# A decoder trunk on one core: the split activations xh and xl in a pool of their own at the far end of SBUF

## Chip, core and metric

The kernel runs on one core of a Trainium2 chip. A core has TensorE (PE; PEld in the profile is its weight load), VectorE (DVE), ScalarE (ACT), GpSimd (POOL) and SyncE (SP), which issues all loads here. On-chip memory (SBUF) has 128 partitions; an address in this text is a byte within each partition. PSUM holds the results of matmuls. The metric is device time in microseconds per execution; lower is better.

## What is computed

Two layers of a decoder with 256 tokens, 1024 features and float32 weights. Each layer is a macaron pair: half a SwiGLU, a token mixer, half a SwiGLU. The mixer of the first layer is attention over dilated windows, that of the second latent attention.

```python
def swiglu(x, w_in, w_out):
    gate, up = jnp.split(x @ w_in, 2, axis=-1)
    return (jax.nn.silu(gate) * up) @ w_out

# each layer
x += 1/2 SwiGLU1(rms(x)); x += mixer(rms(x)); x += 1/2 SwiGLU2(rms(x))
```

`w_in` is 1024 x 5632, `w_out` 2816 x 1024, four of each. The weights are read once; the profile counts 194.14 MB read from HBM.

## The kernel before

Activations stay in SBUF, features on partitions: `xT[p, kt, token]` holds feature kt*128 + p, with KT = 8 chunks of 256 tokens. A product with weights runs as three passes in float32r, since weights and activations are each split into a high and a low part: weights into hi and lo (`piece`, lines 71 to 89: SP loads 1 MB into one of four raw buffers, ACT writes hi, DVE writes lo = raw - hi; three hi and three lo buffers of 8 KB per partition take turns), the activations into xh and xl (`split_x`, lines 100 to 115: ACT writes xh, line 115 on DVE writes xl). xh and xl are two tiles of 8 KB per partition that live through the whole kernel; every layer writes them anew.

Lines 95 to 97 are the three passes: hi with xh, hi with xl, lo with xh. Each matmul has a stationary operand of 128 x 128 (loaded by LDWEIGHTS) and a moving one of 128 x 256.

```python
 64 self.xg = self.xp.tile([P, GCOLS + KT * S], F32, name="xg")
 67 self.xh = self.xp.tile([P, KT, S], F32R, name="xh")
 68 self.xl = self.xp.tile([P, KT, S], F32R, name="xl")
...
 94 for i, (wh, wl, xh, xl) in enumerate(terms):
 95     self.nc.tensor.matmul(out, wh, xh, start=start and i == 0, stop=False, **kw)
 96     self.nc.tensor.matmul(out, wh, xl, start=False, stop=False, **kw)
 97     self.nc.tensor.matmul(out, wl, xh, start=False, stop=stop and i == n - 1, **kw)
...
180 for k in range(KT):
181     for u in range(2):
182         self.mm3(
183             ps[:, u * S : (u + 1) * S],
184             [(hv[:, k, u, :], lv[:, k, u, :], self.xh[:, k, :], self.xl[:, k, :])],
...
432 nc.tensor.matmul(o, self.xh[:, k, ts], hi[:, k, :], start=k == 0, stop=False)
```

- **FFN** (`ffn`, lines 170 to 245). `up(c)` for 22 chunks: 48 matmuls with the weights stationary and xh, xl moving, into a PSUM tile of pool wk (lines 180 to 184). `gate(c)` makes the hidden part h and splits it into hh and hl (pool hh, six buffers each of 1 KB). `down(c)`: 24 matmuls with hh, hl moving, into the PSUM pool acc; two of them follow every second up. `closing` (line 247) ends the down product bank by bank, each followed by the residual and the next split of x.
- **Dilated layer** (`dilated`, line 391): q and k products (lines 418 to 420) with xh, xl stationary and 512 columns of weights moving; v products (lines 432 to 434) with xh, xl stationary and 256 columns moving, into acc; attention; and an output product through lines 95 to 97 with oth, otl moving (`out_product`, line 367), into acc.
- **Latent layer** (`latent`, line 586): an input product through lines 95 to 97 with xh, xl moving, then products from the tiles ch and cl, attention, and an output product with its own oth, otl.

Pools take SBUF in the order in which they are opened, from the low end: const, xp (with xg, xh, xl), raw, hi, lo, st, and behind them the pools of the layer that runs. The Tile framework records the instructions, orders them on each engine and sets the semaphores.

Of the kernel before, what the change touches and what calls it, by code (L numbers as in the profile page):

```python
"""Two-layer hybrid decoder trunk (dilated-window attention, latent attention) on one core.

Activations stay on chip, feature-major: xT[p, kt, token] holds feature kt*128+p.  Products of
float32 operands against the weights run as three float32r passes over an exact split
w = hi + lo (12 significant bits each): hi*xh + hi*xl + lo*xh.  RMS-norm scales are applied
after the products (per token), so a product never waits for a norm's statistics.

The tokens stand even ones first, then odd ones: a dilation of 4 or 16 never joins the two
halves, so those groups' scores are two diagonal blocks.  Only inside the latent layer are they
in their own order, which its input's split and its output's residual turn to and from.  # L10
"""
# [11 lines left out]
F32R = mybir.dt.float32r  # L23
# [6 lines left out]
P = 128  # L30
S = 256
D = 1024
KT = D // P
# [17 lines left out]
class Trunk:  # L51
    def __init__(self, ctx, tc):
        self.tc, self.nc = tc, tc.nc
        e = ctx.enter_context
        self.const = e(tc.tile_pool(name="const", bufs=1))
        self.xp = e(tc.tile_pool(name="xp", bufs=1))
        self.rawp = e(tc.tile_pool(name="rawp", bufs=4))
        self.hip = e(tc.tile_pool(name="hip", bufs=3))
        self.lop = e(tc.tile_pool(name="lop", bufs=3))
        self.st = e(tc.tile_pool(name="st", bufs=2))  # L60
        self.acc = e(tc.tile_pool(name="acc", bufs=4, space=PSUM))
        self.wk = e(tc.tile_pool(name="wk", bufs=3, space=PSUM))
        self.ob = e(tc.tile_pool(name="ob", bufs=1, space=PSUM))
        self.xg = self.xp.tile([P, GCOLS + KT * S], F32, name="xg")
        self.gains = self.xg[:, :GCOLS]
        self.xT = self.xg[:, GCOLS:].rearrange("p (k s) -> p k s", k=KT)
        self.xh = self.xp.tile([P, KT, S], F32R, name="xh")
        self.xl = self.xp.tile([P, KT, S], F32R, name="xl")

    # ---- weights: load a piece, split it exactly into two float32r parts  # L70
    def piece(self, src, cuts=1, before=None):
        """cuts: parts the split is made in; before: called ahead of each part's load, else it's one load."""
        nc = self.nc
# [17 lines left out]
    def mm3(self, out, terms, start, stop, **kw):  # L91
        """out += sum over (wh, wl, xh, xl) of w x; the weight is stationary."""
        n = len(terms)
        for i, (wh, wl, xh, xl) in enumerate(terms):
            self.nc.tensor.matmul(out, wh, xh, start=start and i == 0, stop=False, **kw)  # L95
            self.nc.tensor.matmul(out, wh, xl, start=False, stop=False, **kw)  # L96
            self.nc.tensor.matmul(out, wl, xh, start=False, stop=stop and i == n - 1, **kw)  # L97

    # ---- residual stream
    def split_x(self, d0, xs, in_order=False, shared=False):  # L100
        """Gained x (chunks from d0) as float32r pairs, with the tokens even|odd or in their own order;
        shared: ScalarE and VectorE take turns at the high parts."""
        nc = self.nc
# [13 lines left out]
    def squares(self, d0, xs, in_order=False):  # L117
        """The sum of squares over the chunks."""
        nc = self.nc
# [15 lines left out]
    def residual(self, d0, n, acc, scale, in_order=False):  # L135
        """x += scale * acc for n chunks from d0; acc is their part of a bank, its tokens maybe in order."""
        xs = self.xT[:, d0 : d0 + n, :]
# [9 lines left out]
    def stats(self):  # L147
        """Per-token mean square + eps and its inverse root."""
        nc = self.nc
# [8 lines left out]
    def spread_rstd(self):  # L158
        """The inverse root along the free axis, on every partition."""
        nc = self.nc  # L160
# [7 lines left out]

    # ---- SwiGLU
    def ffn(self, up_w, out_w, finish, start=None, started=None, hook=None):  # L170
# [76 lines left out]
    def closing(self, parts, down, accs, finish, scale):  # L247
        """The last terms of a product bank by bank, each followed by its chunks' residual and split."""
        for d0, cs in parts:
            for c in cs:  # L250
                down(c, (d0, d0 + 1))
            if d0 < KT - 2:
                finish(d0, 2, accs[d0 // 2], scale)
            else:
                for i in range(2):
                    finish(d0 + i, 1, accs[d0 // 2][:, i * S : (i + 1) * S], scale)

    # ---- tables
    def setup_first(self):
# [6 lines left out]
        nc.gpsimd.memset(self.mhalf, -0.5)  # L266
        # the activation table and the PE's clock warm up while the first loads run
        nc.scalar.activation(self.st.tile([P, 2], F32, name="warm"), self.mhalf[:, :2], AF.Silu)
# [4 lines left out]
    def setup(self, cst, pos, gtab):  # L273
        """Masks, and rotary tables with the gains: two token tiles even|odd, two in their own order."""
        nc = self.nc
# [27 lines left out]
        nc.scalar.activation(cos, n, AF.Sin)  # L303
        # A: q gain 0:64, k gain 64:128; B: q gain 128:224, k gain 224:320
        self.tA = k.tile([P, NTT, 2, DA], F32, name="tA")
        self.tB = k.tile([P, NTT, 2, 2, 32], F32, name="tB")
        for tt in range(NTT):
            for qk, sc in ((0, DA**-0.5), (1, 1.0)):
                for hf in range(2):
# [7 lines left out]
                    )  # L317
        # latent attention: q over 96 features, and k's rotary part over 32
        self.tAq = k.tile([P, NTT, QKB], F32, name="tAq")
# [3 lines left out]
        for tt in range(NTT):  # L323
            sc = QKB**-0.5
            # k's gain over the features that aren't rotated goes to q's side of the scores
            nc.vector.scalar_tensor_tensor(
# [12 lines left out]

    # ---- softmax of one score block: probabilities, divided by their sum  # L340
    def softmax(self, p, s, mask):
# [11 lines left out]
    def transposed(self, pool, p, n, name):  # L353
        """n 128-blocks of p, each transposed, in SBUF."""
        nc = self.nc
# [11 lines left out]
    def out_product(self, w_out, oth, otl):  # L367
        """Steps of the output product: part(k, banks)."""
        ws = {}
# [19 lines left out]

    # ---- dilated windows  # L390
    def dilated(self, qk_w, v_w, w_out, finish):
        nc, tc = self.nc, self.tc
        with (
# [63 lines left out]
            def attention(hq, qt, kt, v):  # L457
                """Pipelined steps over (pair of heads, token tile): scores, turned probabilities, outputs."""
                ps, pts, obs = {}, {}, {}
# [54 lines left out]
            for hq in range(4):  # L514
                # group 0's scores are 256 wide: float32r pairs
                qt, kt = (
# [36 lines left out]
    def norm_rope_a(self, at, ps, tt, ee):  # L553
        """Heads of q and k (4 + 4, 64 wide): RMS norm with gains, then rotary embedding."""
        nc = self.nc
# [28 lines left out]

    # ---- latent attention
    def latent(self, in_w, kv_w, q_w, w_out, finish):
        nc, tc = self.nc, self.tc
        with (
# [10 lines left out]
            def in_product(pc):  # L599
# [12 lines left out]
                for i in range(2):  # L612
                    # chunks 0,1: kv rank; 2,3,4: q rank; the rotary key (32 features) comes third
                    c = (0, 1, None, 2, 3, 4)[pc * 2 + i]
# [32 lines left out]
            def mean_square(cs, name):  # L647
                """Per token: mean square of a rank's features + eps, in units of the unscaled ones."""
                ps = self.ob.tile([P, 512], F32, name="ob")
# [16 lines left out]
            def rotary_key():  # L666
                """Token-major: r_x kr', gained and rotated; its square sum."""
                ps = self.ob.tile([P, 512], F32, name="ob")
# [126 lines left out]
    def tok_product(self, out, xh, xl, chunks, tt, wp, cols):  # L795
        """Token-major product: the activations' chunk is stationary."""
        nc = self.nc
# [94 lines left out]

# ---- host: layouts of the inputs, and constants of the shapes
def _layout(i):
# [11 lines left out]
    a["gtab"] = c(np.broadcast_to(gt, (P, gt.size)))  # L906
    # [4, ff chunk, p, (kt, gate|up, 128)]
    w = i["ffn_w_in"].reshape(4, KT, P, 2, NC_FF, P)
    a["up"] = c(w.transpose(0, 4, 2, 1, 3, 5).reshape(4, NC_FF, P, PIECE))
    w = i["ffn_w_out"].reshape(4, NC_FF // 2, 2, P, D)  # L910
    a["down"] = c(w.transpose(0, 1, 3, 2, 4).reshape(4, NC_FF // 2, P, PIECE))
    # [q|k|v][group][quarter][256]
    w = i["a_w_in"][0].reshape(KT, P, 3, GA, 4, S)
# [9 lines left out]
    a["b_out"] = c(i["b_w_out"][0].reshape(4, 2, P, D).transpose(0, 2, 1, 3).reshape(4, P, PIECE))  # L923
    # constants
    ms = []
# [38 lines left out]
```

## Time and profile before

| what | value |
|---|---|
| runs | median 1181.53 us of 3 (1181.19, 1181.53, 1183.71) |
| profiled execution | span 1178.2 us (no other time of it is listed) |
| PE, PEld | busy 1159.9 us (98%), 1106.9 us (94%), 9142 each |
| DVE, ACT, POOL | busy 792.3, 593.1, 102.6 us |
| loads | 196.59 MB, mean 167 GB/s |
| granted TensorE clock | mean 0.998 |

The span runs from the first instruction to the last. Matmuls overlap in the profile: a row of some 280 ns starts some 120 ns behind the one before it, so busy time and mean durations of PE don't say how often one starts. The timeline does, which lists instructions by their start.

### The profile page before, as it was taken

The page shows a single profiled execution, that of the slowest core. Times are in us where ns is not written, and L with a number is a line of the kernel's source. Part 1 is how long each engine was busy: PE and PEld are TensorE (multiplying, and loading weights), DVE is VectorE, ACT ScalarE, POOL GpSimd, SP SyncE. Part 2 cuts the span into 40 slices and gives each one's busy share as a digit, 9 for nine tenths or more (in the row PEclk, how much of TensorE's full clock was granted, in tenths as well). Part 3 has the DMA queues.
Part 4 walks back from the last instruction along what each step waited for, and adds up shares of the span by engine and source line. Part 5 has one row for each costly group of instructions (what it writes and reads, how often), then busy time and mean ns, then how long its engine had stood idle before and what let it go on. Part 6 is the DMA issues. An engine that isn't in the chain of part 4 may idle for free.

```text
span 1178.2 us, 21736 instructions
## 1 busy us (share of the span) xinstructions
PE 1159.9 (98%) x9142; PEld 1106.9 (94%) x9142; DVE 792.3 (67%) x1384; ACT 593.1 (50%) x980; POOL 102.6 (9%) x98
## 2 busy tenths in 40 slices
PE   7999999999999999999999999999999899999998
PEld 7999999888888888999999999999998789999998
DVE  6855557979777776675555676555576897655554
ACT  6444445556555555654444454444466875444441
POOL 2000001212111111200000020000013212000000
PEclk9999999999999999999999999999999999999999
DMA  8655554554444344155555545555533235455540
GB/s 319 216 182 191 191 186 144 214 179 144 141 146 144 112 158 142 56 215 179 184 184 189 192 182 179 179 179 183 184 129 122 108 110 184 175 183 191 192 149 37
DMA packets 29042, 196.59 MB, mean 167 GB/s; under 512 B 3344, under 2 KB 3856, under 8 KB 5904
## 3 DMA queue, kind: packets, MB, share of 16 engines
q1 hardware_dynamic: 28944, 195.21, 47.4%
q8 instruction: 71, 1.16, 0.4%
q14 instruction: 27, 0.22, 0.1%
HBM read 194.14 MB, written 1.05 MB: 166 GB/s over the span
## 4 chain that ended last, share of the span: by engine, by line
PE 90%; DVE 6%; ACT 2%; issue 1%; POOL 1%; DMA 1%; SPq 0%; DVEq 0%; POOLq 0%
PE wk L96 14%; PE wk L97 14%; PE wk L95 14%; PE acc L95 9%; PE acc L97 9%; PE acc L96 9%; PE acc L418 3%; PE acc L420 3%; PE acc L419 3%; PE wk L358 1%; PE acc L432 1%; PE acc L434 1%; DVE lo L88 1%; PE acc L433 1%; PE ob L491 1%; PE wk L446 1%
## 5 line engine op out<-in xcount | busy, mean ns | idle before, releaser
L88 DVE TENSOR_TENSOR lo<-raw,hi 128x512 fp32r<-128x512 f32 (+2 forms) x408 | 447.0, 1119 | 213.2 <-ACT hi L87 211.6
L87 ACT CAST hi<-raw 128x512 fp32r<-128x512 f32 (+2 forms) x408 | 375.2, 963 | 277.2 <-PE wk L96 172.9
L95 PE MATMUL wk<-xh,hi 128*128 128x256 f32 x1408 | 399.8, 284 | 1.6 <-ACT hi L87 1.6
L97 PE MATMUL wk<-xh,lo 128*128 128x256 f32 x1408 | 399.0, 283 | 1.8 <-DVE lo L88 1.8
L96 PE MATMUL wk<-xl,hi 128*128 128x256 f32 x1408 | 398.8, 283 | 0.1
L97 PEld LDWEIGHTS wk<-xh,lo 128*128 128x128 f32 x1408 | 269.9, 192 | 2.6 <-DVE lo L88 2.6
L95 PEld LDWEIGHTS wk<-xh,hi 128*128 128x128 f32 x1408 | 270.1, 192 | 2.2 <-ACT hi L87 2.1
L96 PEld LDWEIGHTS wk<-xl,hi 128*128 128x128 f32 x1408 | 270.0, 192 | 0.8 <-DVE xl L115 0.5
L95 PE MATMUL acc<-hh,hi 128*128 128x256 f32 x704 | 197.2, 280 | 0.0
L97 PE MATMUL acc<-hh,lo 128*128 128x256 f32 x704 | 196.4, 279 | 0.0
L96 PE MATMUL acc<-hl,hi 128*128 128x256 f32 x704 | 196.4, 279 | 0.0
L95 PEld LDWEIGHTS acc<-hh,hi 128*128 128x128 f32 x704 | 132.3, 188 | 0.0
L97 PEld LDWEIGHTS acc<-hh,lo 128*128 128x128 f32 x704 | 132.3, 188 | 0.0
L96 PEld LDWEIGHTS acc<-hl,hi 128*128 128x128 f32 x704 | 131.9, 187 | 0.0
L204 ACT CAST hh<-h 128x256 fp32r<-128x256 f32 x88 | 35.4, 406 | 168.2 <-DVE h L201 168.0
L195 DVE TENSOR_TENSOR gu<-wk,bc 128x512 f32<-128x512 f32 x88 | 60.5, 691 | 76.5 <-PE wk L97 76.2
L418 PE MATMUL acc<-hi,xh 128*128 128x512 f32 x192 | 76.6, 399 | 0.0
L419 PE MATMUL acc<-lo,xh 128*128 128x512 f32 x192 | 75.2, 392 | 0.0
L420 PE MATMUL acc<-hi,xl 128*128 128x512 f32 x192 | 74.9, 390 | 0.0
L205 DVE TENSOR_TENSOR hl<-h,hh 128x256 fp32r<-128x256 f32 x88 | 37.1, 424 | 33.2 <-ACT hh L204 33.1
L562 POOL TENSOR_TENSOR rr<-r,mhalf 128x8 f32<-128x8 f32 x24 | 39.2, 1636 | 205.2 <-DVE r L560 205.2
L130 POOL TENSOR_TENSOR ssq<-sq 128x256 f32<-128x256 f32 x6 | 4.8, 796 | 596.3 <-ACT sq L127 422.0
(183 smaller groups left out, 1521.3 us busy)
## 6 DMA issues: line engine op xcount, KB each, us to landing
raw<-in_up SPq DMA_DIRECT2D x87, 1024.0 KB, 4.8
raw<-in_down SPq DMA_DIRECT2D x44, 1024.0 KB, 4.8
raw<-in_a_qk SPq DMA_DIRECT2D x24, 1024.0 KB, 4.8
raw<-in_a_v SPq DMA_DIRECT2D x12, 1024.0 KB, 4.8
raw<-in_a_out SPq DMA_DIRECT2D x4, 1024.0 KB, 5.4
raw<-in_b_out SPq DMA_DIRECT2D x4, 1024.0 KB, 4.9
raw<-in_b_in SPq DMA_DIRECT2D x3, 1024.0 KB, 4.9
raw<-in_b_q SPq DMA_DIRECT2D x4, 576.0 KB, 3.6
```

The source lines that it names most:

```text
L87: nc.scalar.copy(hi[:, c], raw[:, c])
L88: nc.vector.tensor_tensor(lo[:, c], raw[:, c], hi.bitcast(F32)[:, c], op=ALU.subtract)
L95: self.nc.tensor.matmul(out, wh, xh, start=start and i == 0, stop=False, **kw)
L96: self.nc.tensor.matmul(out, wh, xl, start=False, stop=False, **kw)
L97: self.nc.tensor.matmul(out, wl, xh, start=False, stop=stop and i == n - 1, **kw)
L195: nc.vector.tensor_tensor(gu, ps.rearrange("p (u s) -> p u s", u=2), self.bc.unsqueeze(1).broadcast_to([P, 2, S]), op=ALU.mult)
L204: nc.scalar.copy(hh, h)
L205: nc.vector.tensor_tensor(hl, h, hh.bitcast(F32), op=ALU.subtract)
L418: nc.tensor.matmul(pss[tt], xh, hi[:, k, :], start=kk == 0, stop=False)
L419: nc.tensor.matmul(pss[tt], xh, lo[:, k, :], start=False, stop=False)
L420: nc.tensor.matmul(pss[tt], xl, hi[:, k, :], start=False, stop=kk == KT - 1)
L562: nc.gpsimd.tensor_tensor(rr, r8, self.mhalf[:, :8], op=ALU.pow)
```

## The change

xh and xl move from the pool xp, where they stood behind xg, to a new pool `far` with one buffer, which takes its memory from the far end of the partition (`side="right"`). Comments and docstrings are blanked too, which does nothing; lines behind 67 have their numbers raised by two.

```diff
         self.xT = self.xg[:, GCOLS:].rearrange("p (k s) -> p k s", k=KT)
-        self.xh = self.xp.tile([P, KT, S], F32R, name="xh")
-        self.xl = self.xp.tile([P, KT, S], F32R, name="xl")
+
+        self.far = e(tc.tile_pool(name="far", bufs=1, side="right"))
+        self.xh = self.far.tile([P, KT, S], F32R, name="xh")
+        self.xl = self.far.tile([P, KT, S], F32R, name="xl")
```

Each engine has the same instructions in the same order, with the same waits, before and after. The two built programs differ in addresses (first byte of each buffer within a partition):

| tile | before | after |
|---|---|---|
| const pool, xg | 16512 to 36351 | the same |
| xh | 36352 | 212960 |
| xl | 44544 | 221152 |
| raw (4) | 52736, 60928, 69120, 77312 | 36352, 44544, 52736, 60928 |
| hi (3) | 85504, 93696, 101888 | 69120, 77312, 85504 |
| lo (3) | 110080, 118272, 126464 | 93696, 101888, 110080 |
| hh (6) | 152384 to 158527 | 136000 to 142143 |
| hl (6) | 158528 to 164671 | 142144 to 148287 |
| oth, otl of the dilated layer | 211776, 219968 | 195392, 203584 |
| oth, otl of the latent layer | 188224, 196416 | 171840, 180032 |

[...] PSUM places don't change.

## Rows read from the trace of the kernel before

**Rows 1.** The page's first line, and PE in its part 1 (busy us, share, instructions).
```profile
span 1178.2 us, 21736 instructions
PE 1159.9 (98%) x9142; PEld 1106.9 (94%) x9142; DVE 792.3 (67%) x1384; ACT 593.1 (50%) x980; POOL 102.6 (9%) x98
```

**Rows 2.** The page's part 4: the chain that ended last, by engine and line.
```profile
PE 90%; DVE 6%; ACT 2%; issue 1%; POOL 1%; DMA 1%; SPq 0%; DVEq 0%; POOLq 0%
PE wk L96 14%; PE wk L97 14%; PE wk L95 14%; PE acc L95 9%; PE acc L97 9%; PE acc L96 9%; PE acc L418 3%; PE acc L420 3%; PE acc L419 3%; PE wk L358 1%; PE acc L432 1%; PE acc L434 1%; DVE lo L88 1%; PE acc L433 1%; PE ob L491 1%; PE wk L446 1%
```

**Rows 3.** Waits, ACT's longest: total us, times, longest.
```profile
ACT hi L87 <- PE wk L96: 172.9, 75, 4.3
```

**Rows 4.** Windows: stretch, us, then busy us by engine, clock, DMA share, GB/s.
```profile
core 0: us, PE busy (x) PEld busy (x) DVE busy (x) ACT busy (x) POOL busy (x), PEclk, DMA share, GB/s
0.00:20.00 20.00, 13.88 (x83) 12.51 (x83) 11.03 (x22) 12.34 (x22) 7.03 (x14) 1.00 0.87 317
20.00:190.00 170.00, 170.00 (x1427) 170.00 (x1426) 108.13 (x156) 73.71 (x83) 0.00 (x0) 1.00 0.57 198
```

**Rows 5.** Groups by form: xcount | busy us, mean ns | idle before.
```profile
L95 PE MATMUL wk<-xh,hi 128*128 128x256 f32 x1408 | 399.8, 284 | 1.6 <-ACT hi L87 1.6
...
L95 PEld LDWEIGHTS wk<-xh,hi 128*128 128x128 f32 x1408 | 270.1, 192 | 2.2 <-ACT hi L87 2.1
...
L95 PE MATMUL acc<-hh,hi 128*128 128x256 f32 x704 | 197.2, 280 | 0.0
...
L95 PEld LDWEIGHTS acc<-hh,hi 128*128 128x128 f32 x704 | 132.3, 188 | 0.0
...
L418 PE MATMUL acc<-hi,xh 128*128 128x512 f32 x192 | 76.6, 399 | 0.0
...
L432 PE MATMUL acc<-hi,xh 128*128 128x256 f32 x192 | 55.3, 288 | 0.0
...
L95 PE MATMUL acc<-oth,hi 128*128 128x256 f32 x128 | 37.4, 296 | 0.7 <-DVE kn L818 0.7
...
L95 PE MATMUL acc<-xh,hi 128*128 128x256 f32 x48 | 13.8, 288 | 0.0
```

**Rows 6.** Timeline of PE, a down and two up products: start us, us, instruction.
```profile
122.58 0.28 PE L95 MATMUL acc<-hh,hi 128*128 128x256 f32 x1
...
127.88 0.29 PE L95 MATMUL wk<-xh,hi 128*128 128x256 f32 x1
...
128.60 0.28 PE L95 MATMUL wk<-xh,hi 128*128 128x256 f32 x1
...
139.16 0.28 PE L96 MATMUL wk<-xl,hi 128*128 128x256 f32 x1
```

**Rows 7.** Windows in the up product of rows 6, columns as in rows 4.
```profile
128.60:130.20 1.60, 1.60 (x16) 1.60 (x15) 0.30 (x1) 1.26 (x1) 0.00 (x0) 1.00 1.01 425
130.20:131.80 1.60, 1.60 (x16) 1.60 (x15) 1.60 (x1) 0.00 (x0) 0.00 (x0) 1.00 0.28 118
```

**Rows 8.** Timeline of PE in a v product.
```profile
216.00 0.28 PE L434 MATMUL acc<-hi,xl 128*128 128x256 f32 x1
...
219.24 0.28 PE L434 MATMUL acc<-hi,xl 128*128 128x256 f32 x1
```

**Rows 9.** Timeline of PE in the dilated layer's output product.
```profile
478.44 0.28 PE L95 MATMUL acc<-oth,hi 128*128 128x256 f32 x1
...
480.56 0.28 PE L95 MATMUL acc<-oth,hi 128*128 128x256 f32 x1
```

**Rows 10.** Timeline of PE, a later chunk of the same output product.
```profile
484.89 0.28 PE L97 MATMUL acc<-oth,lo 128*128 128x256 f32 x1
...
485.91 0.28 PE L97 MATMUL acc<-oth,lo 128*128 128x256 f32 x1
```

**Rows 11.** Timeline of PE in a q and k product.
```profile
220.75 0.39 PE L418 MATMUL acc<-hi,xh 128*128 128x512 f32 x1
...
224.15 0.39 PE L418 MATMUL acc<-hi,xh 128*128 128x512 f32 x1
```

**Rows 12.** Groups by form: the instructions that write xl.
```profile
L115 DVE SCALAR_TENSOR_TENSOR xl<-xg,xh 128x256 fp32r<-128x256 f32 x48 | 28.8, 635 | 3.9 <-ACT xh L114 3.9
```

## The prediction

> **What bounds the kernel now.** I read the page from the top. The span is 1178.2 us and TensorE (PE) is busy for 1159.9 us of it [rows 1]. That alone doesn't make PE the bound, so I went to the chain that ended last: 90% of it is PE, and its three longest pieces are lines 95, 96 and 97, the three passes of a product [rows 2]. Then the waits: what ScalarE (ACT) waits for most before it splits a weight piece is PE, to give a `hi` buffer back (172.9 us), so the split stands behind PE and not ahead of it [rows 3]. [...] The time of this kernel is therefore the number of matmuls times the distance from one start to the next, and that distance is what is to be read.
>
> The groups by form give the counts; each form stands there once for its three passes. With 256 moving columns and xh or xl as an operand there are 3 x 1408 in the FFN up products, 3 x 192 in the v products (there xh is the stationary operand) and 3 x 48 in the latent input product, **4944** in all. With hh or hl there are 3 x 704 = 2112, with oth or otl 3 x 128 = 384. With 512 moving columns and xh stationary there are 3 x 192 = 576 [rows 5]. The durations of the matmuls in these rows (280 to 399 ns) overlap and can't be added; only starts tell.
>
> In a down product the starts run from 122.58 to 127.88 us in 45 steps: 5.30/45 = 117.8 ns. In the up products behind it they run from 128.60 to 139.16 us in 88 steps: 10.56/88 = 120.0 ns [rows 6]. The v products, with xh stationary, start 120 ns apart as well: 216.00 to 219.24 us in 27 steps [rows 8]. The output product of the dilated layer, with oth moving, is of the quicker kind: 478.44 to 480.56 us in 18 steps, 117.8 ns [rows 9]. Both kinds take turns through the same three hi and three lo buffers, and read 128 weights and 256 columns on 128 partitions at the same clock. The up product writes another PSUM pool than the down product, but the v product writes the same one and still takes 120. Other engines don't explain it either: in two neighbouring windows of the up stretch DVE goes from 0.30 to 1.60 of 1.60 us and the DMA engines from their full share to 28%, and the 120 ns go on through both [rows 6, 7]. What the slow ones share is xh and xl. Even a weight load is longer beside xh: 192 against 188 ns, from the same hi buffers [rows 5]. One chunk of the output product goes faster still, 484.89 to 485.91 us in 9 steps, 113.3 ns [rows 10]. So three paces are on record, and the middle one belongs to operands that lie elsewhere in memory.
>
> **The change part by part.** By the built programs no instruction is added, removed or moved on any of the five queues (SP's and POOL's among them), and every wait is on the same semaphore with the same value. Only addresses differ. xh goes from byte 36352 to 212960 of each partition, xl from 44544 to 221152; const and xg stay; everything behind them moves down by 16384 bytes, so raw, hi, lo, hh and oth keep their places relative to each other. Before, xh and hi started at the same place modulo 512 bytes, while hh and oth stood 320 bytes off; after, xh stands 480 off, and at 32 modulo 64, where every operand of PE stood at 0 modulo 64 until now. Before, xh and xl were also the only operands of any product with weights below byte 85504. So the change takes away both things that set the slow kind apart, the place and the common offset.
>
> - *The 4944 matmuls with xh or xl.* No row shows xh at its new place. The nearest rows are those of hh and oth, which have the same shape, weights and roles [rows 6, 9]; the oth of rows 9 lies from byte 211776 on, right where xh will be. I take their pace: 120.0 - 117.8 = 2.2 ns less, x 4944 = **10.9 us**. The bounds are 113.3 ns [rows 10], 6.7 ns less, 33.1 us, and on the other side one such step more, 126.7 ns, 33.1 us lost.
> - *The 576 with 512 columns.* They start 226.7 ns apart (220.75 to 224.15 us in 15 steps) [rows 11], 13.3 over the 213.3 ns of their columns. No row shows this form at another pace; between nothing and 576 x 2.2 = 1.3 us, taken as 0.
> - *The 2112 + 384 with hh and oth.* They move down together with hi and lo: 0, as nothing between the operands changes. Bound: back to 120, 2496 x 2.2 = 5.5 us lost.
> - *Writing xh and xl.* The same instructions at other addresses; line 115 has 48 of 635 ns [rows 12]: 0. A tenth more on each would be 3.0 us, most of it beside PE's work.
> - *What could be late next.* An up chunk of 48 steps shrinks from 5.76 to 5.65 us. By rows 4 DVE has 36% of the stretch to spare, ACT 57% and the DMA engines 43%, so no wait takes the gain. In the first 20 us, where PE waits for loads (83 matmuls), 0.2 us of it is lost.
>
> Sum: 10.9 us off. It is made on the profiled execution, whose span is 1178.2 us; that is 3.3 below the median of the runs, 1181.53, and I leave this difference as it is: 1181.5 - 10.9 = **1170.6 us**.
>
> **The rivals.**
>
> *No change (1181.5).* The 120 belongs to something else in these products, or xh falls into it wherever it lies. For it: 120 is 13.3 ns over the 106.7 ns of 256 columns, and the 512-column form is the same 13.3 over its own [rows 11], so 13.3 may be the common toll and 117.8 the exception. Against it: the same hi buffers are read at two paces, and xh and xl alone tell them apart. [...] Chance 0.27.
>
> *Slower, by the new offset (1214.6).* xh and xl will be the only operands that start in the middle of a 64-byte block. [...] If PE is fed by such blocks, 256 columns now touch 17 of them: 4944 x 6.7 = 33.1 us more. It decides as soon as one extra block isn't hidden in the 13.3 ns that a step has beyond its columns. [...] Against it: those 13.3 ns. [...] Chance 0.13.
>
> *Slower, by place (1187.0).* The low addresses are slow for whoever lies there. The hi buffers now begin at 69120 instead of 85504, nearer to where xh was. If the border lies between, x stays at 120 because of its weights, and hh and oth fall to 120 too: 5.5 us more. Chance 0.09.
>
> *Much faster (1148.4).* xh falls into the 113.3 pace: 33.1 us off. For it: rows 10; against it: oth holds that pace in this short stretch only. Chance 0.09.
>
> **How the numbers follow.** A measurement of this kernel can tell some 0.2% (2.4 us) from no change. The forecast has 0.42 and is the likeliest. Faster: 0.42 + 0.09 = 0.51; same: 0.27; slower: 0.13 + 0.09 = 0.22. The range takes in the forecast (its own range is 1168 to 1173: the wide form's 1.3 us below, a fifth of the gain lost above), no change and the smaller slowdown, 0.78 together. Downwards it reaches to 1159, half way to the 113.3 pace, for mixtures of the two. Left out are 126.7 throughout and 113.3 throughout.
>
> **What would show it.** In the profile after, starts in an up product 117.8 ns apart and the weight load beside xh at 188 ns, with down products unchanged: right, and the span about 11 us shorter with the same counts. At 120 and 192: no change. At 127: the offset. Down products at 120: the place. The forecast is wrong as well if the up products quicken and the span doesn't, through idle time of PE in front of lines 95 and 97.

## The result and the profile after

The changed kernel takes **1174.83 us** (median of 4 runs, 1173.87 to 1175.84) against 1181.36 us for the kernel before in the same series: a ratio of 0.9944, 95% interval 0.9927 to 0.9960. That is 6.5 us faster. The forecast was 1170.6 us, with a range from 1159 to past the smaller slowdown of 1187.0: the sign and the place of the gain were right, its size was too large (10.9 us).

The page of the profiled execution (its time 1175.65 us), the first line and PE in part 1. Line numbers are two higher than before.

```profile
span 1173.9 us, 21736 instructions
PE 1154.4 (98%) x9142; PEld 1097.8 (94%) x9142; DVE 793.6 (68%) x1384; ACT 593.0 (51%) x980; POOL 102.9 (9%) x98
```

The counts are those of [rows 1]. DVE and ACT have the same busy time to within 1.3 us; only PE and its weight load lost some. So what changed is how often a matmul starts. The groups by form (xcount | busy us, mean ns | idle before):

```profile
L97 PEld LDWEIGHTS wk<-xh,hi 128*128 128x128 f32 x1408 | 266.5, 189 | 1.8 <-ACT hi L89 1.7
L97 PEld LDWEIGHTS acc<-hh,hi 128*128 128x128 f32 x704 | 132.3, 188 | 0.0
L420 PE MATMUL acc<-hi,xh 128*128 128x512 f32 x192 | 77.6, 404 | 0.0
```

Against [rows 5] the weight load beside xh fell from 192 to 189 ns, beside hh it stayed at 188. The 512-column matmul of the q and k products grew from 399 to 404 ns. The timeline of PE (start us, us, instruction) gives the distances: first and last row of a stretch of down products, of the up products behind it, of a q and k product and of the v product behind that.

```profile
122.65 0.28 PE L97 MATMUL acc<-hh,hi 128*128 128x256 f32 x1
...
128.19 0.28 PE L99 MATMUL acc<-hh,lo 128*128 128x256 f32 x1
128.30 0.28 PE L97 MATMUL wk<-xh,hi 128*128 128x256 f32 x1
...
139.54 0.28 PE L99 MATMUL wk<-xh,lo 128*128 128x256 f32 x1
...
206.17 0.40 PE L420 MATMUL acc<-hi,xh 128*128 128x512 f32 x1
...
212.94 0.40 PE L422 MATMUL acc<-hi,xl 128*128 128x512 f32 x1
...
213.75 0.29 PE L435 MATMUL acc<-lo,xh 128*128 128x256 f32 x1
...
219.12 0.28 PE L436 MATMUL acc<-hi,xl 128*128 128x256 f32 x1
```

- Up: 11.24 us in 95 steps, **118.3 ns** where [rows 6] had 120.0.
- Down: 5.54 us in 47 steps, 117.9 ns, as in [rows 6].
- v: 5.37 us in 46 steps, 116.7 ns where [rows 8] had 120.
- q and k: 6.77 us in 29 steps, **233.4 ns** where [rows 11] had 226.7.

Over the whole trace, pauses left out, the means went from 119.99 to 118.28 ns (up), from 119.81 to 116.96 (v), from 119.8 to 118.3 (latent input), from 227.9 to 233.3 (q and k) and from 117.86 to 117.73 (down). Times the numbers of matmuls: 4224 x 1.71 = 7.2, 576 x 2.85 = 1.6, 144 x 1.5 = 0.2 and 2112 x 0.13 = 0.3 us gained, 576 x 5.4 = 3.1 us lost. The sum is 6.2 us of the measured 6.5.

### The profile page after: what moved, and what is told of

It reads as the page before. It is cut to its first block, busy times and chain, and to the rows that moved or that the text cites. A ratio compares the mean times of both kernels' runs of the same rounds, so it can differ in the third digit from the quotient of the medians.

```text
span 1173.9 us, 21736 instructions
## 1 busy us (share of the span) xinstructions
PE 1154.4 (98%) x9142; PEld 1097.8 (94%) x9142; DVE 793.6 (68%) x1384; ACT 593.0 (51%) x980; POOL 102.9 (9%) x98
## 4 chain that ended last, share of the span: by engine, by line
PE 89%; DVE 7%; ACT 2%; POOL 1%; issue 1%; DMA 1%; SPq 0%; DVEq 0%; POOLq 0%; ACTq 0%
PE wk L98 14%; PE wk L99 14%; PE wk L97 14%; PE acc L97 9%; PE acc L99 9%; PE acc L98 9%; PE acc L420 3%; PE acc L422 3%; PE acc L421 3%; DVE lo L90 2%; PE acc L434 1%; PE wk L360 1%; PE acc L436 1%; PE acc L435 1%; PE ob L493 1%; ACT hi L89 1%
## 5 line engine op out<-in xcount | busy, mean ns | idle before, releaser
L99 PEld LDWEIGHTS wk<-xh,lo 128*128 128x128 f32 x1408 | 266.5, 189 | 3.3 <-DVE lo L90 3.3
L97 PEld LDWEIGHTS wk<-xh,hi 128*128 128x128 f32 x1408 | 266.5, 189 | 1.8 <-ACT hi L89 1.7
L98 PEld LDWEIGHTS wk<-xl,hi 128*128 128x128 f32 x1408 | 266.3, 189 | 0.9 <-DVE xl L117 0.6
```

## The experiments

**Place or offset.** The change moves xh to another place and, with it, to another offset from hi: xh stood 0 bytes behind hi modulo 512 and stands 480 behind it now. Three kernels and a scan take the two apart.

*far_0*: the changed kernel with padding in its pool, so that the place stays and the offset goes back to 0.

```diff
         self.far = e(tc.tile_pool(name="far", bufs=1, side="right"))
         self.xh = self.far.tile([P, KT, S], F32R, name="xh")
         self.xl = self.far.tile([P, KT, S], F32R, name="xl")
+        self.pad = self.far.tile([P, 120], F32, name="pad")
```

> xh and xl stay at the far end, but start 480 bytes lower (212480), so that they begin at the same place modulo 512 as hi and lo, as they did before the change. Place theory (the low end of SBUF was slow): up products keep the quicker pace of about 118.3 ns, time as after the change, about 1174.8 us. Offset theory (equal starts modulo 512 lock the step at 120 ns): up products back at 120.0 ns and 192 ns per weight load, time back at about 1181.4 us.

Measured: 1181.34 us, ratio 1.0000 (0.9991 to 1.0009). Timeline of PE, up products of far_0:

```profile
130.79 0.29 PE L98 MATMUL wk<-xh,hi 128*128 128x256 f32 x1
...
142.19 0.28 PE L100 MATMUL wk<-xh,lo 128*128 128x256 f32 x1
```

11.40 us in 95 steps are 120.0 ns again. At the new place and the old offset nothing is gained, so the place is worth nothing.

*near_480* and *near_320*: the kernel before with xh and xl where they were, moved by padding of 480 or 320 bytes, and the rest of 512 behind them. Their diff, for 480 (80 and 48 for near_320):

```diff
+        self.pad = self.xp.tile([P, 120], F32, name="pad")
         self.xh = self.xp.tile([P, KT, S], F32R, name="xh")
         self.xl = self.xp.tile([P, KT, S], F32R, name="xl")
+        self.pad2 = self.xp.tile([P, 8], F32, name="pad2")
```

> xh and xl stay in their old pool at the low end, with 480 bytes of padding ahead and 32 behind, so that they stand 480 bytes off hi and lo modulo 512, as after the change. Place theory: up products stay at 120.0 ns, about 1181.4 us. Offset theory: up products at about 118.3 ns, v products at about 117, q and k products slowed to some 231 ns, time about 1174.8 us.

> xh and xl at the low end, 320 bytes off hi and lo modulo 512, which is where hh and oth stand and where they took 117.8 ns before. Place theory: 120.0 ns, 1181.4 us. Offset theory: up products at 117.8 ns, 0.5 ns less than after the change, which over 4224 matmuls is 2 us: about 1173 us, if the q and k products don't slow further.

Measured: near_480 1175.33 us, ratio 0.9954 (0.9941 to 0.9966); near_320 1172.48 us, ratio 0.9929 (0.9916 to 0.9941). Timelines of PE, up products, first of near_480, then of near_320:

```profile
128.03 0.28 PE L97 MATMUL wk<-xh,hi 128*128 128x256 f32 x1
...
139.26 0.28 PE L99 MATMUL wk<-xh,lo 128*128 128x256 f32 x1
```

```profile
127.68 0.28 PE L97 MATMUL wk<-xh,hi 128*128 128x256 f32 x1
...
138.87 0.28 PE L99 MATMUL wk<-xh,lo 128*128 128x256 f32 x1
```

95 steps take 11.23 us (118.2 ns) and 11.19 us (117.8 ns). Without the new pool, 480 bytes give the changed kernel's paces, and 320, the offset that hh and oth had all along, gives their 117.8 ns. The offset is the cause. (hi starts at 0 modulo 512 bytes in all these kernels, so that the offset is also xh's own address modulo 512; *mixed_offsets* below takes these two apart in part.)

*offset_scan*: streams of 96 matmuls in the forms of the kernel, each behind a short pause, at 19 offsets and, for the up form, at ten places of its moving operand.

> A kernel of matmul streams alone, none of the model's work: the forms of the up, v and q/k products, each with 96 (48 for 512 columns) matmuls from idle, for 19 offsets of xh and xl against hi and lo (0 to 480 in steps of 32, and 8, 16, 48), then the up form at 10 places across SBUF with offsets 0 and 480. Offset theory: 120.0 ns at offset 0 at every place, other values at other offsets, the same at every place; at 480 about 118.3 (up), 117 (v), 231 (q/k, against 226.7 at 0). Place theory: the pace depends on the place, and not on the offset. If only starts off a 64-byte multiple matter, 32, 96, 160 and so on differ from 64, 128, 192.

In its timeline each stream is one row (start us, length us, form, count, pause ahead). First the up form at 96, 192, 256 and 320, then the q and k form with its stationary operand at 0, 32, 64 and 192, then the up form at offsets 0 and 480 at the lowest and at the highest of the ten places:

```profile
53.47 11.79 PE L43 MATMUL ps<-z 128*128 128x256 f32 x96 [0.73 <-ACT res L40]
...
90.76 11.16 PE L43 MATMUL ps<-z 128*128 128x256 f32 x96 [0.73 <-ACT res L40]
...
115.01 11.78 PE L43 MATMUL ps<-z 128*128 128x256 f32 x96 [0.73 <-ACT res L40]
...
139.71 11.15 PE L43 MATMUL ps<-z 128*128 128x256 f32 x96 [0.73 <-ACT res L40]
...
481.55 11.20 PE L43 MATMUL ps<-z 128*128 128x512 f32 x48 [0.52 <-ACT res L40]
493.48 11.47 PE L43 MATMUL ps<-z 128*128 128x512 f32 x48 [0.73 <-ACT res L40]
505.68 11.47 PE L43 MATMUL ps<-z 128*128 128x512 f32 x48 [0.73 <-ACT res L40]
...
554.47 11.26 PE L43 MATMUL ps<-z 128*128 128x512 f32 x48 [0.73 <-ACT res L40]
...
712.19 11.78 PE L43 MATMUL ps<-z 128*128 128x256 f32 x96 [0.73 <-ACT res L40]
724.70 11.62 PE L43 MATMUL ps<-z 128*128 128x256 f32 x96 [0.73 <-ACT res L40]
...
935.87 11.78 PE L43 MATMUL ps<-z 128*128 128x256 f32 x96 [0.73 <-ACT res L40]
948.38 11.62 PE L43 MATMUL ps<-z 128*128 128x256 f32 x96 [0.73 <-ACT res L40]
```

The place does nothing: 11.78 and 11.62 us at both ends. The offset does, and 256 is as slow as 0. Over the second half of each stream the up form takes 120.0 ns at 0 and 256, but 119.9 to 120.1 at 96, 352 and 8 too, so a common offset isn't the only slow one. It takes 113.3 at 192 and 320, 118.4 at 224 and 480, and between 116.6 and 118.7 at all others. The v form takes 120.0 at 0 and 256, at 160 and 416 too, and 115.6 (at 8) to 118.6 elsewhere. The q and k form is best at 0 and 256, where the others are among their worst: 226.7 ns there, 228.7 at 192 and 448, 230.6 to 234.1 elsewhere. VectorE does nothing from the second stream on, and ScalarE only copies out between streams: in 9.6 us within the streams at 192 and 256 (from 92.0 and from 116.0 us) PE runs 87 and 82 matmuls, VectorE, ScalarE and GpSimd are busy for 0.00 us, and the DMA share is 0.01. The effect needs no other engine: it lies in the places of PE's own two operands.

**Which offset is worth having.** *near_192* and *near_256* are near_320 with other padding (48 and 80 float32, 64 and 64).

> xh and xl stay at the near end, 192 bytes behind hi modulo 512 (48 float32 of padding ahead of xh, 80 behind xl; nothing else moves by other than 512 bytes). Theory of the offset, by the scan of matmuls alone: up products at 117.8 ns or, if they hold the quicker of two paces, 113.3; v products 117.8; q and k products 228.8 instead of 226.7. Sum from 1181.4: 4224 x 2.2 + 576 x 2.2 - 576 x 2.1 = 9.3 us less, 1172 us; with the up products at 113.3 it would be 1153. If only the far offsets 320 and 480 help and 192 does not, the up products stay at 120 and the time at 1181 or, with the slower q and k products, 1182.5.

> As near_192, with xh and xl 256 bytes behind hi modulo 512 (64 float32 of padding on either side). If what counts is the offset modulo 256, this is a common offset again: up and v products 120.0, q and k products 226.7, the time of the kernel before, 1181.4 within 2. If any offset other than 0 modulo 512 helps, up products at 118 to 119 and the time 1174 to 1178.

Measured: near_192 **1155.22 us**, ratio 0.9784 (0.9769 to 0.9800); near_256 1181.15 us, ratio 0.9995 (0.9985 to 1.0005). The windows show two stretches of 120 us, in the first and in the third FFN; what counts is PE's (x...), the matmuls that run in it, those begun just before it among them. Columns are as in [rows 4]. The kernel before and near_256, each in the first FFN, then near_192 in both:

```profile
60.00:180.00 120.00, 120.00 (x1008) 120.00 (x1007) 68.46 (x63) 49.91 (x50) 0.00 (x0) 1.00 0.53 184
```

```profile
60.00:180.00 120.00, 120.00 (x1008) 120.00 (x1007) 68.44 (x63) 49.98 (x49) 0.00 (x0) 1.00 0.54 185
```

```profile
60.00:180.00 120.00, 120.00 (x1021) 120.00 (x1021) 68.61 (x64) 51.20 (x50) 0.00 (x0) 1.00 0.55 187
720.00:840.00 120.00, 120.00 (x1046) 120.00 (x1045) 71.54 (x66) 51.49 (x52) 0.00 (x0) 1.00 0.56 191
```

An offset of 256 gains nothing: 1008 matmuls, as before. At 192 the first FFN does 1021, with its up products at 117.7 ns, and the third does 1046, with its up products at 113.4, at the same clock of 1.00 and with the same addresses. So the offset alone doesn't fix the pace; at 192 two are possible, and something else chooses. (This trace is of the slowest of near_192's four executions, 1158.92 us. The other three took 1154.88 to 1155.54; no row shows their first FFN, which may have run at the other pace.)

*pace_memory* asks what.

> Leaves the whole network out: only streams of matmuls, its output is not the reference's. Streams of 96 up-like matmuls (256 columns, offsets between moving and stationary operand of 0, 64, 192, 320, 448, 480 bytes modulo 512) follow one another without idle time, in pairs; at 192 and 320 also from idle, with down-like streams, and after single matmuls of other widths. If the pace belongs to the offset alone, every stream at 192 and 320 runs at 113.3 ns, as from idle in the offset scan, whatever ran before it. If the pace is a state that is carried over, streams at 192 and 320 run at 113.3 after some predecessors and at 117.8 after others, and a single matmul of another width between two streams may change it.

Windows of pace_memory (columns as above): a stream at 192 behind one at 0, one at 192 behind one at 64, and one at 192 behind one at 320.

```profile
49.00:58.60 9.60, 9.60 (x87) 9.60 (x86) 0.00 (x0) 0.00 (x0) 0.00 (x0) 1.00 0.01 2
...
139.00:148.60 9.60, 9.60 (x84) 9.60 (x83) 0.00 (x0) 0.00 (x0) 0.00 (x0) 1.00 0.01 2
...
240.00:249.60 9.60, 9.60 (x87) 9.60 (x87) 0.00 (x0) 0.33 (x1) 0.00 (x0) 1.00 0.01 2
```

By their starts, 87 in a window are a pace of 113.3 ns and 84 one of 117.8. Every stream at 192 right behind one at 0 ran at 113.3, the one behind 64 at 117.8 to its end. The one stream at 320 in the scan, behind a pause, ran at 113.3; here, without such pauses, streams at 320 ran at 117.8 in all but one case. So the pace is a mode: past its first few matmuls each stream kept its own, 113.3 or 117.8 ns, to its end. What a single matmul of another width between two streams does to the mode is not shown.

*all_192* is near_192 with a third padding, a pool of 96 float32 behind `st`, by which hh, hl, oth and otl also stand at 192. *all_192_reset* adds 16 matmuls at offset 0 in the first FFN:

```diff
                     wo(c // 2)
+                    if c == 5 and start:
+                        for _ in range(16):
+                            nc.tensor.matmul(accs[3][:, :S], wos[0][0][:, 0, S : S + P], wos[0][0][:, 0, :S], start=True, stop=True, skip_group_check=True)
                     if c < NC_FF - 1:
                         down(c - 3)
```

> near_192 with a further 96 float32 (384 bytes) of padding behind the pool st, so that hh, hl, oth and otl too stand 192 bytes behind hi and lo modulo 512 instead of 320. Theory (offset sets which paces are possible, and which of the two holds is carried on from one matmul to the next): down products at 113.4 ns in the FFNs whose up products have that pace, 4.4 ns x 528 less in each, three of four in near_192: 7 us less than near_192's 1155.2, 1148; 1142 if the first FFN falls into 113.3 as well, 1164 and more if a second one stays at 117.8 throughout. Rival (the pace belongs to the role of hh, or each stretch chooses afresh): down products stay at 117.8 and the time at 1155.

> all_192 with 16 more matmuls in the first FFN, ahead of its first down product, whose two operands both come from one hi buffer, 0 bytes apart modulo 512; their result is overwritten. 16 x 120 ns = 1.9 us more work. If the pace is carried on and a stretch at offset 0 throws it back, as every stream at 192 behind one at 0 ran at 113.3 in the run of streams, the first FFN goes on at 113.4 instead of 117.8 behind them: some 864 up and 528 down matmuls x 4.4 = 6.1 us less, 4 us net below all_192 if that one's first FFN stays at 117.8, and 2 us above it if it doesn't. If the pace is chosen afresh at each stretch, 2 us above all_192 in any case.

Measured: all_192 1164.64 us, ratio 0.9855 (0.9840 to 0.9870); all_192_reset 1169.51 us, ratio 0.9898 (0.9881 to 0.9914). (The 16 matmuls of all_192_reset change what one accumulator holds; the number and form of all others are those of all_192.) Windows of all_192 (early in the first FFN, then the two stretches), of all_192_reset (the first two of these), and timeline of its 16 matmuls:

```profile
24.00:47.00 23.00, 23.00 (x205) 23.00 (x204) 20.84 (x71) 12.83 (x23) 0.00 (x0) 1.00 0.77 286
60.00:180.00 120.00, 120.00 (x1062) 120.00 (x1061) 71.30 (x65) 52.47 (x51) 0.00 (x0) 1.00 0.56 194
720.00:840.00 120.00, 120.00 (x1021) 120.00 (x1021) 69.80 (x64) 50.23 (x49) 0.00 (x0) 1.00 0.54 185
```

```profile
24.00:47.00 23.00, 23.00 (x198) 23.00 (x197) 20.04 (x70) 9.68 (x18) 0.00 (x0) 1.00 0.76 279
60.00:180.00 120.00, 119.94 (x1018) 119.74 (x1017) 70.09 (x65) 50.43 (x50) 0.00 (x0) 1.00 0.56 193
```

```profile
47.18 0.87 PE L243 MATMUL acc<-hi 128*128 128x256 f32 x6
...
48.33 0.76 PE L243 MATMUL acc<-hi 128*128 128x256 f32 x5
...
54.35 0.77 PE L243 MATMUL acc<-hi 128*128 128x256 f32 x5
```

My forecast of 1148 us for all_192 fell by sign: it is 9 us slower than near_192. But it shows the mode plainly. Now all products of an FFN have one offset, and from its first down product on a whole FFN runs in one mode: the first at 113.3, up and down alike, the other three at 117.8. In near_192 the down products, at 320 and 117.8 ns, had stood between the up products without spoiling them in three FFNs of four.

The reset tested less than it was meant to. Its 16 matmuls did not run as one stretch, but as groups of 6, 5 and 5 with up products between them, behind the first down products and not ahead of them; the mode stayed at 117.8. But another thing came out. Ahead of the first group PE has the same 314 matmuls in the same order in both kernels, from the same addresses, and yet from 24 us on all_192 ran them at 113.3 ns and all_192_reset at 117.8. So the matmuls and their addresses together don't fix the mode either.

**A combination without the slow mode.** *mixed_offsets* gives the three passes offsets of their own.

> Leaves the whole network out: only streams of up-like matmuls, its output is not the reference's. The three passes get offsets of their own (hi with xh, hi with xl, lo with xh): 20 combinations, each as a stream of 96 behind 48 at offset 64 (which left 192 at 117.8 ns in the run before) and again behind 48 at offset 0 (which left it at 113.3). Then 48 at 64, 48 at 192, n at 0 for n from 1 to 96, and 96 at 192. If the pace is a mode that is carried on, 192 throughout runs at 117.8 behind 64 and at 113.3 behind 0, and some length of n is needed to change it: 16 did not do it in all_192_reset, so more than 16 here. If a mixed combination breaks the mode, it runs at one pace behind both: at 113.3 it would be worth having in the kernel, at 117.8 or above not.

Windows of mixed_offsets: first 192 for both passes with hi and 64 for the pass with lo, behind a stream at 64 and behind one at 0; then 128 for the pass with lo, behind 64; then 192 throughout, behind 2 and behind 16 matmuls at 0.

```profile
53.00:62.60 9.60, 9.60 (x87) 9.60 (x86) 0.00 (x0) 0.02 (x1) 0.00 (x0) 1.00 0.00 0
69.50:79.10 9.60, 9.60 (x87) 9.60 (x87) 0.00 (x0) 0.19 (x1) 0.00 (x0) 1.00 0.00 0
86.00:95.60 9.60, 9.60 (x84) 9.60 (x83) 0.00 (x0) 0.26 (x1) 0.00 (x0) 1.00 0.00 0
...
727.50:737.10 9.60, 9.60 (x84) 9.60 (x84) 0.00 (x0) 0.00 (x0) 0.00 (x0) 1.00 0.01 2
...
797.40:807.00 9.60, 9.60 (x87) 9.60 (x86) 0.00 (x0) 0.27 (x1) 0.00 (x0) 1.00 0.01 2
```

Of 20 combinations only (192, 192, 64) and its like (192, 192, 320), besides 192 throughout, ran at 113.3 behind both predecessors. 192 throughout behind 64 ran at 113.3 eight times and at 117.8 twice, so its choice isn't made by the predecessor's offset alone. Behind 8 or more matmuls at 0 it ran at 113.3 in all six cases, behind 1, 2 or 4 at 117.8. My expectation of more than 16 took the 16 of all_192_reset for one stretch; its groups of 5 and 6 lie between the 4 and the 8 of this run and don't contradict it. What chooses the mode stays open.

The combinations also show that the weights' address counts, and not that of xh alone: with xh and xl in place and only lo moved, (192, 192, 64) ran at 113.3 ns and (192, 192, 128) at 118.0 to 118.5. That only the difference of the two addresses counts, and not each one's own place modulo 512, is not shown: hi keeps one place modulo 512 in all runs. Nor do good offsets add up: (192, 320, 320) took 120 to 122 ns.

*lo_shift* puts (192, 192, 64) into the kernel: all_192 with lo moved by 128 bytes.

```diff
+        self.lgap = e(tc.tile_pool(name="lgap", bufs=1))
         self.lop = e(tc.tile_pool(name="lop", bufs=3))
...
-        self.pad3 = self.gap.tile([P, 96], F32, name="pad3")
+        self.pad3 = self.gap.tile([P, 64], F32, name="pad3")
+        self.pad4 = self.lgap.tile([P, 32], F32, name="pad4")
```

> all_192 with lo alone moved by 128 bytes (32 float32 of padding ahead of it, 32 fewer behind st): hi with xh and hi with xl stay 192 bytes apart modulo 512, lo with xh becomes 64, and the same for hh and oth. In the run of mixed offsets this combination ran at 113.3 ns behind both predecessors, 64 and 0, with the same steps each time. If it breaks the mode that holds 117.8, the up and down products of all four FFNs run at 113.3: 4752 matmuls of the later three FFNs x 4.45 = 21 us less than all_192, 1143 to 1144; the v, q and k products, whose moving operand changes its offset with lo, can move this by 3 either way. If the streams alone mislead (the other engines or the pauses of the kernel matter), one or more FFNs stay at 117.8: 7 us more for each, 1150 to 1165.

Measured: **1144.02 us** (1142.54 to 1144.85), ratio 0.9690 (0.9677 to 0.9704), the fastest of all. Page, windows, and timeline of an up and a down product:

```profile
span 1140.8 us, 21736 instructions
PE 1122.7 (98%) x9142; PEld 1068.6 (94%) x9142; DVE 792.6 (69%) x1384; ACT 594.0 (52%) x980; POOL 102.3 (9%) x98
```

```profile
60.00:180.00 120.00, 120.00 (x1062) 120.00 (x1061) 71.75 (x66) 52.53 (x51) 0.00 (x0) 1.00 0.56 194
720.00:840.00 120.00, 120.00 (x1061) 120.00 (x1060) 73.58 (x70) 53.26 (x57) 0.00 (x0) 1.00 0.57 195
```

```profile
597.30 0.28 PE L101 MATMUL wk<-xh,hi 128*128 128x256 f32 x1
...
608.07 0.28 PE L103 MATMUL wk<-xh,lo 128*128 128x256 f32 x1
608.18 0.28 PE L101 MATMUL acc<-hh,hi 128*128 128x256 f32 x1
...
611.92 0.28 PE L101 MATMUL acc<-hh,hi 128*128 128x256 f32 x1
```

95 steps of up in 10.77 us are 113.4 ns, 33 of down in 3.74 us are 113.3; every FFN runs at these paces from its first down product on. The same 9142 matmuls take 37 us less than before, in the same order, with nothing changed but addresses.

All full kernels but all_192_reset together (mean distance of starts over each trace in ns, pauses left out; offset of xh behind hi modulo 512):

| kernel | offset | us | up | v | q, k | down |
|---|---|---|---|---|---|---|
| before | 0 | 1181.4 | 120.0 | 119.8 | 227.9 | 117.9 |
| after | 480 | 1174.8 | 118.3 | 117.0 | 233.3 | 117.7 |
| far_0 | 0 | 1181.3 | 120.0 | 119.8 | 228.0 | 117.9 |
| near_480 | 480 | 1175.3 | 118.3 | 117.0 | 233.3 | 117.7 |
| near_320 | 320 | 1172.5 | 117.8 | 114.7 | 233.3 | 117.8 |
| near_256 | 256 | 1181.2 | 120.0 | 119.8 | 228.0 | 117.9 |
| near_192 | 192 | 1155.2 | 114.9 | 116.7 | 229.4 | 117.8 |
| all_192 | 192 | 1164.6 | 116.6 | 117.8 | 229.4 | 116.7 |
| lo_shift | 192 (lo: 64) | 1144.0 | 113.4 | 117.6 | 230.4 | 113.4 |

## Why the prediction was right, and where it was off

- *The bound.* Right: the time is the number of matmuls times the distance of their starts. PE's rows changed, the other engines' didn't.
- *The 4944 matmuls, 10.9 us.* This is the term that was mis-sized. "I take their pace", 117.8 from hh and oth, took over the pace of an offset of 320 for an offset of 480. The text had both numbers and named the common offset as one of two candidates, but didn't ask what another offset than 320 gives. The up products gained 1.7 ns instead of 2.2, the v products 2.85: 9.0 us together. That 480 came so near to 320 was in part luck. The place, which was the prediction's other reason to take oth's pace, proved worth nothing, and in the scan the up form gains nothing at offsets of 96 and 352.
- *The 576 with 512 columns, taken as 0.* Wrong by sign, and the bounds, from nothing to a gain of 1.3 us, left out a loss. They lost 3.1 us: at offset 0 this form had its best pace, 226.7 ns. The row was seen in one state only, and a bound on both sides would have had to allow 6.7 ns more as well. No row shows the prediction's 106.7 ns for 256 columns, 213.3 for 512 and 13.3 over them by themselves; as an estimate they follow from two paces, 226.7 - 120.0 = 106.7 ns for 256 columns more [rows 6, 11]. In the scan at an offset of 192 this difference is 228.7 - 113.3 = 115.4 ns, so a toll common to all paces is not shown.
- *The forecast's own range, 1168 to 1173.* The 1174.8 measured lies above it. Its lower end doesn't follow from its terms: 1.3 us below 1170.6 is 1169.3.
- *hh and oth, the writes, and what is late next, all 0.* Right: down products at 117.9 ns, DVE and ACT busy as before, and the span less PE's busy time went from 18.3 to 19.5 us only.
- *No change.* It fell, though it takes far_0 and near_256 to see how near it was: at offsets of 0 and 256 the gain is nothing, and in the scan at 96 and 352 neither. Other engines left the pace alone: PE kept its 120 ns while DVE went from 0.30 to 1.60 us of 1.60 and the DMA share from 1.01 to 0.28 [rows 6, 7]. But the two operands don't leave each other alone: with DVE idle, the up form took 113.3 or 120.0 ns in offset_scan by their offset, and in mixed_offsets 113.3 or 118.0 to 118.5 when only lo was moved.
- *Slower by the new offset.* No run shows a step of 6.7 ns for a further block of 64 bytes: a matmul with 256 columns went from 120.0 to 118.3 ns in the up products. 6.7 ns were added to one with 512, but the scan has 233.3 ns for it at an offset of 64 too (its row at 505.68), so a cut 64-byte block is not the reason.
- *Slower by place.* It fell with far_0: hi at its lower place, and 120.0 and 117.9 ns as before.
- *Much faster.* The 113.3 pace is no accident of a stretch. The change just doesn't reach it in the products with xh; near_192 does in three FFNs, lo_shift in all.

## What to carry to other kernels

Where PE is the bound and starts come 12% slower than the estimate for their columns alone (120.0 against 226.7 - 120.0 = 106.7 ns, from [rows 6, 11]), compare the addresses of the moving and the stationary operand modulo 512 bytes: 0 and 256 were among the slowest offsets for 256 columns here, with 96 and 352 (119.9 to 120.1 ns in the up form, against 113.3 at 192 and 320), and padding of under 1 KB per partition took 3.1% off the whole kernel. Scan the offsets for every form of matmul apart, since the form with 512 columns preferred the offset that is worst for 256 (226.7 ns at 0, 228.7 to 234.1 at all others but 256). Then try the winner in the kernel itself, because a pace that a stream holds alone may not be the one that the kernel falls into (at 320 the scan had 113.3 ns and near_320 117.8).

## What was not expected of the hardware

- The distance of matmul starts (128 stationary columns, float32r, clock 1.00) depends on the places of the two operands modulo 512 bytes, alike at offsets of 0 and 256, and not on where in the partition they lie: 120.0 or 118.4 ns at all ten places. 8 bytes change nothing in the up form (120.0), 16 do (118.7); in the v form 8 bytes give its best pace (115.6).
- At some offsets two paces are possible, 113.3 and 117.8 ns, and either was kept for over 100 us by one kernel with one set of addresses. all_192 and all_192_reset took different ones in the same matmuls from the same addresses. What picks one at the start of a stretch is not settled. The times can repeat nevertheless: all_192, with one FFN in the one mode and three in the other, stayed between 1162.46 and 1165.36 us in its 4 runs.
- Why the two operands' offset matters was not measured. A common offset alone doesn't account for it: the up form took 120.0 ns at 0 and 256, but 119.9 to 120.1 at 96, 352 and 8 as well.
